# Eight of sixteen output tiles of w_out by one level of Strassen, in a fused transformer block on one Trainium2 core

## The chip, the cores and the metric

The kernel runs on one NeuronCore of one Trainium2 chip. The metric is the device time of one execution in microseconds. Five engines run side by side, each in the order of its own queue, and wait for one another through semaphores: TensorE (PE, matmuls; PEld its weight loads), VectorE (DVE), ScalarE (ACT), GpSimd (POOL, here used almost only to issue DMAs) and SyncE (SP, which only issues DMAs). All DMAs of the core run on its 16 DMA engines.

## The reference

A decoder block on 512 tokens with 2048 features, all in float32:

```python
x = x + jnp.concatenate([o_nsa, o_gla], axis=-1) @ w_out      # 2048 x 2048
hq = rms_norm(x, g_cross)
...                                                           # cross attention, 4 heads, 256 memory tokens
hf = rms_norm(x, g_ffn)
gg, uu = jnp.split(hf @ w_gu, 2, axis=-1)
return x + (jax.nn.silu(gg) * uu) @ w_down
```

`o_nsa` are eight sparse-attention heads and `o_gla` four gated linear-attention heads of two rows each: sixteen blocks of 128 features, the "mixed heads", which w_out projects back to 2048 features.

## The kernel before

**Precision.** Every large product is made of float32r matmuls on operands split in two: `split` writes hi = the rounded value (ACT) and lo = the rest (DVE). `mm3` then issues three matmuls, hi x hi, hi x lo and lo x hi, so a 128x128 block of weights against 512 tokens is three matmuls of 512 columns, each with its own weight load. All matmuls of helpers stand at one line, L109, and all splits at L196.

**Order of the program.** Memory keys and values, the projections of the combined input with the heads of both groups running between them, w_out, cross attention, then the feed-forward, whose two products (w_gu, w_down) already use one level of Strassen. A class `Flows` runs the heads as generators beside the projections: `tick()` counts one step, one every two contraction blocks of a projection, and resumes whatever is due. The order on each engine is then set by the framework's scheduler.

**Sums in DRAM.** Strassen needs sums of weight quarters. For w_down (`td`) and the first block of w_gu (`gu0`) POOL makes them in DRAM: a DMA copies a quarter, later ones add into it (`accum_op`). These are 120 DMAs in `turns`, sorted by a number that spreads each family, and given to the ticks 70 to 576 evenly. Each waits for the last matmul issued before its tick (L152 to L176), so POOL's queue runs in step with PE. `spill` and the loads of mixed heads are in the same queue.

**w_out.** `mixp` holds the sixteen mixed heads split, in 32 rows of the tag X. Heads that were spilled are loaded back in rows KS (L1057). L1070 projects the sixteen output tiles one by one: a tile is 16 contraction blocks x 3 = 48 matmuls, its weights two halves of 128x1024, each loaded by SP (4 raw buffers `w`) and split (3 buffers `wh`, 3 `wl`). L1080 adds the tile to x (`xs[m]`), L1085 and L1086 square it and add the square to `ss`, and `split_row` multiplies by g_cross and splits the row (`x1g`, L198 and L199) for the next projection, w_cq. The memory keys (`ckt`, `ckp`) are loaded and split at tiles 4 and 8. After w_out, `cross_norm` sums `ss` over features with PE, and `cross_head` runs four heads.

## Time and profile before

| | |
|---|---|
| median of three runs | 2292.02 us (2290.96 to 2294.07) |
| profiled execution | 2292.03 us, its span 2290.2 us |
| PE, DVE, ACT busy | 2281.0, 1653.3, 1179.4 us |
| heads end, w_out (729 to 891 us) | PE busy all of 162 us, DVE 68, ACT 51 |
| cross attention (891 to 915 us) | PE 23.83 of 24, DMA share 0.24 |

A busy time is the union of the engine's instructions; matmuls overlap in the pipeline, so their spacing is read from their starts. A row of a group gives count, busy time, mean ns of one, and the idle time before them with what ended it. In the chain of waits, the work that ended last is followed back, and its shares say which engine the program waited for. Times of the views are microseconds from the start of the span.

### The profile page before, as it was taken

Reading aid. Unit: us, or ns where it says so; the run is one execution under the profiler, and the core shown is the slowest. Engines: PE = TensorE matmul, PEld = TensorE weight load, DVE = VectorE, ACT = ScalarE, POOL = GpSimd, SP = SyncE. Lnnn points to the kernel's source line nnn. Section 1 sums busy time; section 2 is a strip of 40 time slices with the busy share of each in tenths; the row PEclk is TensorE's granted clock in tenths of the full one; section 3 lists DMA queues with packets and bytes.
Section 4 is the critical chain, followed back from the end, with each engine's and each line's share of the span. In section 5 each row is a group of like instructions: output and inputs, shape, how many; then the busy total and the mean of one; then the engine's idle time right before and its main releaser. Section 6 shows DMA issues by size and latency. Waiting matters only on the chain.

```text
span 2290.2 us, 29462 instructions
## 1 busy us (share of the span) xinstructions
PE 2281.0 (100%) x10800; PEld 1894.1 (83%) x10800; DVE 1653.3 (72%) x2525; ACT 1179.4 (51%) x1802; POOL 149.7 (7%) x200
## 2 busy tenths in 40 slices
PE   9999999999999999999999999999999999999999
PEld 7898888888887888788888888888888888888887
DVE  7548886666778335588788778878887886775685
ACT  7534454556667224475455445544554565444442
POOL 0011121111112110020000000000000000000000
PEclk9999999999999999999999999999999999999999
DMA  8587677856559773295445545543554497767674
GB/s 300 175 209 184 157 188 208 220 159 151 156 142 276 209 188 100 89 271 193 148 142 188 166 136 168 179 161 125 174 175 142 160 339 265 246 235 249 233 248 147
DMA packets 143441, 435.22 MB, mean 190 GB/s; under 512 B 14688, under 2 KB 35808, under 8 KB 140352
## 3 DMA queue, kind: packets, MB, share of 16 engines
q1 hardware_dynamic: 90832, 329.69, 42.4%
q0 software_dynamic: 28896, 79.18, 15.8%
q10 hardware_dynamic: 23568, 24.47, 3.0%
q8 instruction: 84, 1.38, 0.2%
q14 instruction: 61, 0.50, 0.1%
HBM read 394.75 MB, written 101.45 MB: 217 GB/s over the span
## 4 chain that ended last, share of the span: by engine, by line
PE 95%; DVE 2%; DMA 1%; ACT 1%; issue 1%; SPq 0%; ACTq 0%; DVEq 0%
PE mm L109 50%; PE t L109 18%; PE s L109 14%; PE o L109 11%; PE t L988 1%; PE s L1366 1%; DMA raw<-w_gu 1%; DVE wl L196 0%; DVE ql L196 0%; DMA st<-x_t 0%; PE t L1556 0%; ACT wh L196 0%; DMA PH<-w_ck 0%; ACT e L1129 0%; PE t L976 0%
## 5 line engine op out<-in xcount | busy, mean ns | idle before, releaser
L196 ACT CAST qh<-raw 128x1024 fp32r<-128x1024 f32 (+1 forms) x494 | 477.9, 976 | 513.8 <-PE o L109 168.7
L196 DVE TENSOR_TENSOR ql<-raw,qh 128x1024 fp32r<-128x1024 f32 (+1 forms) x494 | 553.7, 1127 | 145.9 <-PE mm L109 55.6
L109 PE MATMUL mm<-X,wh 128*128 128x512 f32 x1664 | 525.1, 395 | 0.0
L109 PEld LDWEIGHTS mm<-X,wh 128*128 128x128 f32 x1664 | 305.4, 188 | 60.0 <-issue 2.2
L109 PE MATMUL t<-qh,PB 128*128 128x512 f32 x968 | 334.9, 391 | 0.0
L109 PE MATMUL mm<-X,wl 128*128 128x512 f32 x832 | 326.2, 392 | 0.2
L196 DVE TENSOR_TENSOR wl<-w,wh 128x1024 fp32r<-128x1024 f32 (+2 forms) x172 | 205.8, 1202 | 163.3 <-ACT wh L196 162.6
L196 ACT CAST wh<-w 128x1024 fp32r<-128x1024 f32 (+2 forms) x172 | 176.6, 1032 | 270.3 <-PE mm L109 177.1
L109 PE MATMUL mm<-qh,PB 128*128 128x512 f32 x868 | 309.8, 389 | 0.0
L109 PE MATMUL s<-qh,PB 128*128 128x512 f32 x672 | 232.6, 391 | 0.6 <-ACT qh L196 0.6
L109 PE MATMUL mm<-qh,PA 128*128 128x512 f32 x640 | 221.5, 389 | 0.0
L109 PEld LDWEIGHTS t<-qh,PB 128*128 128x128 f32 x968 | 181.7, 188 | 37.1
L109 PEld LDWEIGHTS mm<-qh,PB 128*128 128x128 f32 x868 | 163.0, 188 | 34.0 <-ACT qh L196 0.2
L109 PE MATMUL t<-ql,PB 128*128 128x512 f32 x484 | 188.3, 389 | 0.0
L109 PE MATMUL o<-qh,PB 128*128 128x512 f32 x484 | 187.4, 389 | 0.0
L109 PEld LDWEIGHTS mm<-X,wl 128*128 128x128 f32 x832 | 156.2, 188 | 34.0 <-DVE wl L196 1.5
L109 PE MATMUL mm<-ql,PB 128*128 128x512 f32 x434 | 169.0, 389 | 0.1
L109 PEld LDWEIGHTS s<-qh,PB 128*128 128x128 f32 x672 | 126.0, 188 | 26.8 <-ACT qh L196 1.3
L109 PEld LDWEIGHTS mm<-qh,PA 128*128 128x128 f32 x640 | 120.1, 188 | 25.2
L109 PE MATMUL s<-ql,PB 128*128 128x512 f32 x336 | 131.4, 391 | 0.1
L109 PE MATMUL mm<-ql,PA 128*128 128x512 f32 x320 | 124.5, 389 | 0.0
L1299 DVE TENSOR_TENSOR raw<-raw 128x1024 f32<-128x1024 f32 x80 | 96.9, 1220 | 17.7 <-DMA raw<-w_gu 17.7
(486 smaller groups left out, 3388.3 us busy)
## 6 DMA issues: line engine op xcount, KB each, us to landing
raw<-w_gu SPq DMA_DIRECT2D x80, 768.0 KB, 4.1
raw<-w_down SPq DMA_DIRECT2D x88, 512.0 KB, 4.7
raw<-w_gu SPq DMA_DIRECT2D x80, 512.0 KB, 3.5
td<-w_down POOLq DMA_DIRECT2D x66, 512.0 KB, 7.1
w<-w_a SPq DMA_DIRECT2D x60, 512.0 KB, 5.8
raw<-td SPq DMA_DIRECT2D x22, 1024.0 KB, 5.0
HR<-h SPq DMA_DIRECT2D x35, 512.0 KB, 4.9
h<-T ACTq DMA_DIRECT2D x66, 256.0 KB, 3.7
```

Source lines behind the costliest of these rows:

```text
L109: last_mm[0] = PE.matmul(*args, **kw)
L196: last_split[:] = S.copy(hi, src), V.tensor_sub(lo, src, hi)
L988: PE.transpose(tp[:, 128 * (i - j):128 * (i - j) + 128], ps_[b][:, POFF[i] + 128 * j:POFF[i] + 128 * j + 128], ident)
L1299: V.tensor_add(raw[:, 0:1024], raw[:, 0:1024], raw[:, 512:1536])
L1366: PE.transpose(ps[f][:, 128 * i:128 * i + 128], hs[i][:, c:c + 128], ident)
```

## The change

The first eight output tiles are projected as before (`w_o8`). The last eight form two units, u = 2 and 3, of four tiles each. In a unit the contraction (blocks in pairs, the even and the odd head of a pair), the output tiles (pairs) and the tokens (halves of 256) are each cut in two, and seven products replace eight: product `a` takes one quarter of the weights, plain or summed, for two output tiles `i`, against one quarter or sum of quarters of the mixed heads, 256 tokens wide. Results gather in four PSUM banks (`b1`, `b2`, `b3`, `bu`); products 1, 6 and 2 add on to what a bank holds, after `add_22` has read it.

The weight quarters come in a new layout, `w_out`, of four tiles in DRAM with quarters side by side. Their sums (`wo`) are made in DRAM by POOL, 32 more DMAs in `turns`, which now has 152 entries over the ticks 70 to 600. The four sums of the mixed heads (`fac`) are made on chip: every mixed head is spilled, `load_mixes` loads a pair of blocks back on POOL's queue, `mix_sums` makes the sums on DVE and splits them. The places of `mixp`, `fac` and `x1g` are shared by a table (`PLACE`); the x1g rows of the first eight tiles are made during the units, and the memory keys are loaded after the units and split in the first cross head. Heads 4 and 5 use rows st in place of M and are spilled and loaded back too.

```diff
+FIRST_SUM, LAST_SUM = 70, 600
+    wo = [dram.tile([128, 4096], F32, name="wo", tag="wo", bufs=4) for b in range(4)]
+    def add_half(b, h, k):
+        d, w = wo[b][:, 2048 * h:2048 * h + 2048], w_out[b, :, 2048 * h:2048 * h + 2048]
+        def go():
+            if k == 0:
+                i = G.dma_start(d, w)
+            else:
+                dst, src = ((d[:, 512:1536], w[:, 1024:2048]), (d[:, 1536:2048], d[:, 512:1024]),
+                            (d[:, 0:512], d[:, 1536:2048]))[k - 1]
+                i = G.dma_start(dst, src, accum_op=OP.add, max_dma_last_dim=2048)
...
-    turns += [((4 * kp + k + 0.9) / (4 * KP), add_block(kp, k)) for kp in range(KP) for k in range(4)]
+    turns += [((4 * kp + 5.1 * k + 0.9) / (4 * KP + 16), add_block(kp, k)) for kp in range(KP) for k in range(4)]
+    turns += [((2 * b + h + 1.3 * k + 0.2) / 14.5, add_half(b, h, k)) for b in range(4) for h in range(2) for k in range(4)]
...
+    def factor_of(a, kp):
+        if a < 3:
+            return part(mixp[2 * kp + (a > 0)], 256 * (a == 2), 256)
+        return part(fac[a, kp // 2], 256 * (kp % 2), 256)
+    def load_mixes(*kps):
+        for kp in kps:
+            mixes[kp] = [row(tag) for tag in (("M", "rs") if kp % 2 else ("n", "ss"))]
+            for h in range(2):
+                G.dma_start(mixes[kp][h], saved[MIX_ORDER[2 * kp + h]])
+    def mix_sums(*kps):
+        for kp in kps:
+            a0, a1, b0, b1 = [t[:, 256 * i:256 * i + 256] for t in mixes[kp] for i in range(2)]
+            for a, op, d, x, y in ((3, V.tensor_sub, b1, b1, a1), (5, V.tensor_sub, a1, a0, a1),
+                                   (4, V.tensor_add, a0, b1, a0), (6, V.tensor_sub, b0, a0, b0)):
+                op(d, x, y)
...
+                split(*factor_of(a, kp), d)
...
+    def out_weights(src):
+        with tc.high_priority(offset=OUT_AHEAD):
+            raw = sb([128, 1024], "w", 4)
+            nc.sync.dma_start(raw.rearrange("p (h c) -> p h c", h=2), src)
+            hi, lo = sb([128, 1024], "wh", 3, F32R), sb([128, 1024], "wl", 3, F32R)
+            split(hi, lo, raw)
+    def unit(u, a):
+        q, dst, summed = {0: (3, b1, 0), 1: (0, b1, 0), 3: (2, b3, 1), 5: (1, b2, 1), 4: (3, bu, 1), 6: (1, b3, 0),
+                          2: (0, b2, 1)}[a]
...
+        for i in range(2):
+            b = 2 * u - 4 + i
+            w = out_weights((wo[b] if summed else w_out[b])...[:, :, 512 * q:512 * q + 512])
+            for kp in range(KP):
+                mm3(dst[u][:, 256 * i:256 * i + 256], part(w, 128 * kp, 128), factor_of(a, kp), ...)
+                if kp % 4 == 3:
+                    flows.tick()
...
+    def add_22(u):
+        n = ns[u] = spare_n[u % 2]
+        V.tensor_sub(n, bu[u], us[u])
+        V.tensor_sub(t, n, b2[u])
+        V.tensor_sub(t, t, b3[u])
...
+    def finish_x1(u, *ks):
+        for k in ks:
+            m = 4 * u + k
...
+            split(*x1g[m], xs[m], vec("g_cross", m))
+            if m:
+                sq = sqs[k % 2]
+                S.activation(sq, xs[m], AF.Square)
+                V.tensor_add(ss, ss, sq)
...
-    for m in range(KT):
-        ps = project(Weights(w_out[m], 2048), mixp)
...
+    for m in range(8):
+        V.tensor_add(xs[m], project(Weights(w_o8[m], 2048), mixp), xs[m])
+        for at, go, g in ((2, load_mixes, 0), (3, mix_sums, 0), (3, load_mixes, 1), (5, mix_sums, 1),
+                          (5, load_mixes, 2), (6, mix_sums, 2)):
+            if m == at:
+                go(2 * g, 2 * g + 1)
+    for u in (2, 3):
+        unit(u, 0)
+        us[u] = row("M")
+        S.copy(us[u], b1[u])
+    load_mixes(6, 7)
+    unit(2, 1)
+    add_11(2)
+    mix_sums(6, 7)
...
+    unit(2, 3)
+    finish_x1(0, 0, 1)
+    unit(3, 3)
+    finish_x1(0, 2, 3)
+    unit(2, 5)
+    finish_x1(1, 0, 1)
+    unit(2, 4)
+    finish_x1(1, 2, 3)
+    unit(3, 5)
+    for u in (2, 3):
+        add_22(u)
+        unit(u, 6)
+        add_n(u)
+        add_21(u)
+        if u == 3:
+            finish_x1(3, 1, 3)
+        unit(u, 2)
+        add_12(u)
+        if u == 2:
+            unit(3, 4)
+            unit(3, 1)
+            finish_x1(2, 1, 3, 0, 2)
+            add_11(3)
+    finish_x1(3, 0, 2)
```

Three places show how the order moves. On PE, at the end of the eighth output tile, the next tile of 512 columns stood before (X are mixed heads, one hi and one lo row each; mm is a bank):

```order
L109 MATMUL mm_7586<-X_7034,wh_7582 128x512
L109 MATMUL mm_7586<-X_7035,wh_7582 128x512
L109 MATMUL mm_7586<-X_7034,wl_7583 128x512
L109 MATMUL mm_7656<-X_6974,wh_7646 128x512
L109 MATMUL mm_7656<-X_6975,wh_7646 128x512
L109 MATMUL mm_7656<-X_6974,wl_7647 128x512
L109 MATMUL mm_7656<-X_6978,wh_7646 128x512
```

Now unit 2's first product stands there, 256 columns wide, over every second head:

```order
L110 MATMUL mm_7694<-X_7076,wh_7690 128x512
L110 MATMUL mm_7694<-X_7077,wh_7690 128x512
L110 MATMUL mm_7694<-X_7076,wl_7691 128x512
L110 MATMUL mm_7746<-X_7016,wh_7749 128x256
L110 MATMUL mm_7746<-X_7017,wh_7749 128x256
L110 MATMUL mm_7746<-X_7016,wl_7750 128x256
L110 MATMUL mm_7746<-X_7024,wh_7749 128x256
```

Three matmuls per block stay three, at half the columns, and each still brings its own weights.

On POOL, the DRAM sums of the time around the eighth tile's end stood alone before (td for w_down, gu_112 for w_gu):

```order
L173 DMA gu_111<-gu_111 128x512
L154 DMA td<-td 128x2x512
L156 DMA td<-w_down 128x1024
L169 DMA gu_112<-w_gu 16x16384
L154 DMA td<-td 128x2x512
```

Now a load of a spilled mixed head (M) stands between them; it belongs to the last two block pairs, and the td row ahead of it is the sum of tick 530:

```order
L191 DMA wo<-wo 128x512
L155 DMA td<-td 128x2x512
L157 DMA td<-w_down 128x1024
L155 DMA td<-td 128x2x512
L157 DMA td<-w_down 128x1024
L155 DMA td<-td 128x2x512
L1103 DMA M<-spill 128x512
L174 DMA gu_112<-gu_112 128x512
```

The last sum of `wo` stands six rows ahead of that load.

On DVE, in w_out before, a tile's addition, a square's addition and two weight splits alternate:

```order
L196 TENSOR_TENSOR wl_7653<-w_7650,wh_7652 128x1024
L1080 TENSOR_TENSOR KV_7056<-mm_7586,KV_7056 128x512
L196 TENSOR_TENSOR wl_7724<-w_7721,wh_7723 128x1024
L1086 TENSOR_TENSOR ss_7070<-ss_7070,n_7637 128x512
L196 TENSOR_TENSOR wl_7730<-w_7727,wh_7729 128x1024
```

In the units, the last mix (rs, M), its split (X_7947), the rows of x1g (X_8043) and the additions out of a bank (KV, on) stand between the weight splits:

```order
L215 TENSOR_TENSOR wl_7983<-w_7980,wh_7982 128x1024
L215 TENSOR_TENSOR X_7962<-ss_7875,X_7961 128x256
L218 SCALAR_TENSOR_TENSOR X_8043<-KV_7090,vecs_117,X_8042 128x512
L1110 TENSOR_TENSOR rs_7879<-rs_7879,M_7878 128x256
L215 TENSOR_TENSOR wl_8014<-w_8011,wh_8013 128x1024
L215 TENSOR_TENSOR X_7947<-rs_7879,X_7946 128x256
L1110 TENSOR_TENSOR M_7878<-M_7878 128x256
L218 SCALAR_TENSOR_TENSOR X_8048<-q1_7110,vecs_117,X_8047 128x512
L1159 TENSOR_TENSOR KV_7086<-mm_7746,KV_7086 128x256
L1159 TENSOR_TENSOR on_7112<-mm_7746,on_7112 128x256
L215 TENSOR_TENSOR wl_8057<-w_8054,wh_8056 128x1024
```

The weight split wl_8014 and all behind it now stand behind the subtraction that needs the M load.

More of the change, by code (lines that the diff above doesn't have):

```diff
@@ L63, in hybrid_block @@
 def hybrid_block(ctx: ExitStack, tc: tile.TileContext, x_t, mem_t, sv, cmat, umask, w_a, w_r67, w_v, w_vg, w_v3,
-                 w_vsw, w_gk2, w_c1, w_c2, w_out, w_cq, w_ck, w_cv, w_co, w_gu, w_down, y_t):
+                 w_vsw, w_gk2, w_c1, w_c2, w_o8, w_out, w_cq, w_ck, w_cv, w_co, w_gu, w_down, y_t):
     nc = tc.nc
@@ L1007, in nsa_head @@
         done.add(("a", h))
-        t = row("st" if h < 4 else "M")
+        t = row("st" if h < 6 else "M")
         S.copy(t, o)
@@ L1015, in nsa_head @@
         V.scalar_tensor_tensor(t, t, vec("g_nsa"), r, op0=OP.mult, op1=OP.mult)
-        mix[h] = spill(t) if h < 4 else t
+        saved[h] = spill(t)
+        mix[h] = saved[h] if h < 6 else t
     us = short_rows(10)
@@ L1035, in swish_gate @@
         V.tensor_mul(r1, r1, e)
-        V.tensor_mul(t, t, r1)
-        mix[8 + m] = spill(t) if m < 6 else t
+        d = t if m < 6 else row("M")
+        V.tensor_mul(d, t, r1)
+        saved[8 + m] = spill(d)
+        mix[8 + m] = saved[8 + m] if m < 6 else d
     for n in IN_ORDER:
@@ new lines, in hybrid_block @@
+    b1, b2, b3, bu, us, ns = {}, {}, {}, {}, {}, {}
+    def unit(u, a):
+        q, dst, summed = {0: (3, b1, 0), 1: (0, b1, 0), 3: (2, b3, 1), 5: (1, b2, 1), 4: (3, bu, 1), 6: (1, b3, 0),
+                          2: (0, b2, 1)}[a]
+        again = a in (1, 6, 2)
+        if not again:
+            dst[u] = bank({0: "mm", 3: "s", 5: "t", 4: "o"}[a])
+        for i in range(2):
+            b = 2 * u - 4 + i
+            w = out_weights((wo[b] if summed else w_out[b]).rearrange("p (h c) -> p h c", h=2)
+                            [:, :, 512 * q:512 * q + 512])
+            for kp in range(KP):
+                mm3(dst[u][:, 256 * i:256 * i + 256], part(w, 128 * kp, 128), factor_of(a, kp),
+                    start=not again and kp == 0 and i == 0, stop=kp == KP - 1 and i == 1, again=again)
+                if kp % 4 == 3:
+                    flows.tick()
@@ new lines, in columns, with add_11 @@
+    def columns(u):
+        for i in range(2):
+            yield xs[4 * u + 2 * i], xs[4 * u + 2 * i + 1], slice(256 * i, 256 * i + 256)
+    T0, T1 = slice(0, 256), slice(256, 512)
+    def add_11(u):
+        for x, _, c in columns(u):
+            V.tensor_add(x[:, T0], b1[u][:, c], x[:, T0])
+    spare_n, t = [row("on"), row("on")], row("q1")
+    def add_22(u):
[3 more added lines that the diff above has]
+        V.tensor_sub(t, t, b3[u])
@@ new lines, in add_n, with add_21, add_12 @@
+    def add_n(u):
+        for x, y, c in columns(u):
+            V.tensor_add(y[:, T0], y[:, T0], ns[u][:, c])
+            V.tensor_sub(x[:, T1], x[:, T1], ns[u][:, c])
+            V.tensor_add(y[:, T1], y[:, T1], t[:, c])
+    def add_21(u):
+        for _, y, c in columns(u):
+            V.tensor_sub(y[:, T0], y[:, T0], b3[u][:, c])
+    def add_12(u):
+        for x, _, c in columns(u):
+            V.tensor_add(x[:, T1], b2[u][:, c], x[:, T1])
+    ss = row("M")
+    x1g = [None] * KT
@@ L1090, in hybrid_block, with memory_keys @@
+    finish_x1(3, 0, 2)
+    ckt, cv = [row("X") for _ in range(2)], [row("X") for _ in range(2)]
+    for i in range(2):
+        G.dma_start(ckt[i], memkv["k", i])
+        G.dma_start(cv[i], memkv["v", i])
+    ckp = []
+    def memory_keys():
+        for a in range(2):
+            ckp.append(split_row(ckt[a]))
     oc = []
@@ L1349, in phase @@
             weights(kp)
+            flows.tick()
             for p in last if kp == KP - 1 else middle:
```

67 lines of the change are left out of this document (38 added, 29 removed).

## The prediction

> **What bounds the kernel now.** I read the first part of the page, then the chain of waits, then the table by stage.
>
> ```profile
> span 2290.2 us, 29462 instructions
> PE 2281.0 (100%) x10800; PEld 1894.1 (83%) x10800; DVE 1653.3 (72%) x2525; ACT 1179.4 (51%) x1802; POOL 149.7 (7%) x200
> PE 95%; DVE 2%; DMA 1%; ACT 1%; issue 1%; SPq 0%; ACTq 0%; DVEq 0%
> 729.00:775.00 46.00, 46.00 (x203) 37.64 (x202) 19.93 (x24) 14.59 (x18) 8.42 (x10) 1.00 0.89 233
> 775.00:820.00 45.00, 45.00 (x201) 37.26 (x200) 14.97 (x16) 10.54 (x12) 6.64 (x8) 1.00 0.75 202
> 820.00:860.00 40.00, 40.00 (x178) 33.15 (x177) 13.75 (x15) 9.85 (x12) 6.41 (x8) 1.00 0.71 189
> 860.00:891.00 31.00, 31.00 (x140) 25.56 (x138) 19.31 (x25) 16.16 (x23) 0.85 (x1) 1.00 0.45 114
> ```
>
> TensorE is the bound: 95% of the chain is PE work. The last four rows are the w_out stage, columns PE, PEld, DVE, ACT, POOL (busy us and count), granted clock, DMA share, GB/s. PE has no idle time there, the clock is full, and DVE and ACT are under half busy until the last 31 us. So a matmul that disappears here shortens the program by its spacing, as long as nothing new starves PE.
>
> A busy time of 0.39 us is not the spacing of pipelined matmuls; that is read from start to start.
>
> ```profile
> 98.48 0.40 PE L109 MATMUL t<-wh,X 128*128 128x256 f32 x2
> 112.87 0.40 PE L109 MATMUL t<-wh,X 128*128 128x256 f32 x2
> 879.80 0.39 PE L109 MATMUL mm<-X,wl 128*128 128x512 f32 x1
> 890.68 0.39 PE L109 MATMUL mm<-X,wl 128*128 128x512 f32 x1
> 887.03 0.69 DVE L1080 TENSOR_TENSOR KS<-mm,KS 128x512 f32<-128x512 f32 x1
> ```
>
> The first pair lies 40 groups of three matmuls apart, all 256 wide, each with its own weight load, in the same hi-hi-lo pattern: 14.39 / 120 = 0.120 us each. The second pair lies 16 groups of three apart, 512 wide: 10.88 / 48 = 0.2267 us. One output tile of w_out has 48 of these, 10.88 us. The last row evicts the sixteenth tile, so that tile ends at 886.9 and the eighth at 886.9 - 8 x 10.88 = 799.9.
>
> **The matmuls.** The last eight tiles go: 8 x 48 = 384 at 0.2267 = 87.0 us. In come two units of seven products; a product is 2 tiles x 8 pairs of contraction blocks x 3 = 48 matmuls of 256, 5.76 us: 672 at 0.120 = 80.6 us. That is 6.4 us less. Seven eighths would be 10.9 us less; 4.5 us of it goes because half-width matmuls cost 53% and not 50%. Everything else can only take away from 6.4.
>
> **Feeding the units.** Before, a half tile of weights lasts PE 5.44 us; now it lasts 24 x 0.120 = 2.88. The stage needs 28 loads and splits of 128x1024 in 80.6 us, where 16 stood in 87.0.
>
> ```profile
> L196 DVE TENSOR_TENSOR wl<-w,wh 128x1024 fp32r<-128x1024 f32 (+2 forms) x172 | 205.8, 1202 | 163.3 <-ACT wh L196 162.6
> L196 ACT CAST wh<-w 128x1024 fp32r<-128x1024 f32 (+2 forms) x172 | 176.6, 1032 | 270.3 <-PE mm L109 177.1
> 710.50 0.42 DVE L196 TENSOR_TENSOR PL<-t,PH 128x256 fp32r<-128x256 f32 x1
> 709.78 0.35 ACT L196 CAST PH<-t 128x256 fp32r<-128x256 f32 x1
> 883.64 3.39 DVE L199 SCALAR_TENSOR_TENSOR X<-KV,vecs,X 128x512 fp32r<-128x512 f32 x5
> 890.10 0.69 DVE L1086 TENSOR_TENSOR ss<-ss,n 128x512 f32<-128x512 f32 x1
> ```
>
> DVE in the 80.6 us: 28 x 1.20 = 33.6 for the weights; the mixes of the last two block pairs, 8 sums and 8 splits at 0.42 = 6.7; per unit three 512-wide ops at 0.69 and twelve 256-wide at 0.42, together 14.2; sixteen x1g splits at 0.68 and fifteen additions of squares at 0.69 = 21.2. Sum 75.7 us, 94%; it was about a third of the time. ACT: 28 x 1.03 + 8 x 0.35 + 34 ops of 512 at about 0.65 = 54 us. DVE fits, with 5 us to spare, but it runs in order: what waits for a product holds the weight splits behind it, and only three split halves (8.6 us) stand before PE. Bounds 0 and 5 us.
>
> The same for DMA.
>
> ```profile
> q0 software_dynamic: 3515, 9.18, 36.1%
> q1 hardware_dynamic: 3200, 11.61, 29.4%
> w<-w_out SPq DMA_DIRECT2D x15, 512.0 KB, 4.5
> q0 software_dynamic: 2217, 6.06, 53.7%
> q1 hardware_dynamic: 2444, 6.52, 39.4%
> w<-w_out SPq DMA_DIRECT2D x9, 512.0 KB, 6.3
> td<-td POOLq DMA_DIRECT2D x4, 512.0 KB, 11.3
> q0 software_dynamic: 3649, 9.70, 56.4%
> q1 hardware_dynamic: 2624, 9.13, 30.9%
> w<-w_a SPq DMA_DIRECT2D x17, 512.0 KB, 8.0
> ```
>
> The DMA view of 770 to 890, then of 720 to 770 (four rows), the last three of 130 to 220; q0 is POOL's queue of DRAM sums, q1 SP's weights. From the first two rows half a megabyte costs 120 x 0.361 / 17.5 = 2.5 us of all 16 engines on q0 and 120 x 0.294 / 22.1 = 1.6 us on q1. The units ask for 28 x 1.6 = 44.6 us of weights (55%), and the DRAM sums, one per 3.49 ticks instead of 4.22, for about 15 x 2.5 = 37 us (46%). That is 101%: the transfers run full. What helps is depth: four raw buffers, so a half comes every (landing + 1.03 + 1.20) / 4 us, and 2.88 is kept up to a landing of 9.3 us. The median landing was 8.0 under a share of 87% (130 to 220) and 6.3 under 93% (720 to 770). Bounds 0, and at a landing of 11 us 28 x 0.43 less the 8.6 us that stand split, 3.4 us. The DMA and DVE limits overlap; I take 0.6 us for both, near the rows of 6.3 and 8.0, which cost nothing.
>
> **The mixes on POOL's queue.** Sixteen loads of mixed heads are new, in order among the sums, each of which waits for PE's tick. One is late: the M row of the last two block pairs, behind the sum due at tick 530.
>
> ```profile
> 801.74 1.19 POOL L154 DMA_DIRECT2D td<-td  x1 [5.06 <-PE mm L109]
> 807.05 0.54 POOL L156 DMA_DIRECT2D td<-w_down  x1 [4.12 <-PE mm L109]
> 744.12 1.16 POOL L173 DMA_DIRECT2D gu<-w_gu  x1 [13.86 <-issue]
> 761.22 1.14 POOL L154 DMA_DIRECT2D td<-td  x1 [14.21 <-PE mm L109]
> KS<-spill POOLq DMA_DIRECT2D x8, 256.0 KB, 3.5
> st<-spill POOLq DMA_DIRECT2D x6, 256.0 KB, 7.5
> ```
>
> The 807.05 row is the 110th of 120 sums, due at tick 529; a tick of w_out is 1.36 us, so the eighth tile ends at tick 524. In the units a tick is 12 x 0.120 = 1.44 us: tick 530 comes 8.6 us after the eighth tile, the td issue takes 1.2, M's own 0.5, and the load lands 3.5 to 7.5 us later (last two rows, 640 to 720): 13.8 to 17.8 us. The fourth product's first half needs the sum made from it at 17.28 + 2.52 = 19.8, less a subtraction, a cast, a split and their handovers, 1.5 us: 18.3. So there is 0.5 to 4.5 us of slack if POOL is on time. Its queue was 14 us behind at 744 and 761, and on time from 784 on. If late, ACT and DVE both stand at this mix with the weight splits behind them, and PE follows one for one. I take 0.5 us; bounds 0 and 11.
>
> **Ends and covers.** The sum of squares must now wait for two additions, two splits and two squares after the last product; DVE order puts a weight split between: 2 x 0.42 + 1.20 + 2 x (0.68 + 0.69) and handovers, about 5.2 us, where PE has 22 matmuls, 5.0 us, in front of it. Before it waited 0.19 us:
>
> ```profile
> 890.84 0.97 PEld L109 LDWEIGHTS s<-vecs,ss 128*128 128x128 f32 x8 [0.19 <-DVE ss L1086]
> 640.00:729.00 89.00, 88.91 (x463) 72.66 (x461) 73.64 (x191) 67.69 (x144) 19.73 (x30) 1.00 0.72 200
> ```
>
> I take 0.3 (0 to 1.3). The mixes of the first block pairs are made among the heads, 16 DVE ops of 0.42 and 8 casts for a pair of them, where DVE is 83% and ACT 76% busy; PE's order there is unchanged and its idle 0.1 us in 89, so 0.2 (0 to 1.5). Splitting the memory keys in the first cross head instead of under w_out is 2 x 0.68 on DVE under 10.9 us of the next w_cq tile: 0.1 (0 to 0.5). The other mixes, the eight DRAM tiles' 32 sums and the extra spills cost nothing before 800 us while the weights there last 5.44 us per half; without that cover they are the rivals below.
>
> **Sum.** -6.4 + 0.6 + 0.5 + 0.3 + 0.2 + 0.1 = -4.7 us. The profiled execution took 2292.03, its span 2290.2 and 1.8 around it; it stands at the median of 2292.02. Span 2285.5, time 2287.3.
>
> **Rivals.** (1) Weights late, chance 0.18: DMA at 101% lets landings reach 10 to 12 us, PE waits 3 to 6 us at every second product, the gain is gone: about 2290, no change. For it the sum of demands, against it 720 to 770, where 93% cost PE nothing.
>
> (2) M late, the case on the other side, chance 0.18: the POOL queue is still behind when the eighth tile ends, since between the first w_out tile and tick 530 it has 23 sums where 19 stood, and twelve mixes. Behind by the 14 us of the 744.12 row, M lands 9.5 to 13.5 us late and the time is -5.2 + 11.5 = 6.3 over, 2298. It decides from a landing 18.3 us after the eighth tile, and turns slower at about 23.5. Against it: at 801 and 807 POOL waited for PE, not for the ring.
>
> (3) Weight loads pace the narrow matmuls, 0.02. Each unit matmul has a load that takes 188 ns:
>
> ```profile
> L109 PEld LDWEIGHTS mm<-X,wh 128*128 128x128 f32 x1664 | 305.4, 188 | 60.0 <-issue 2.2
> ```
>
> At that spacing 672 x 0.188 = 126.3, 39 us over 87.0: 2331. The 0.120 above, with as many loads, speaks against it. The Trainium skill (TensorE: Matmul & The Clock Gate, section Back-to-back issue gap) says that loads and matmuls together set the spacing, 81 ns at 128 columns and 131 at 512; read as a straight line that is some 98 at 256, 75% of a full one, and as an estimate the units would then take 113.7 us and the time rise by 27 to 2319. The trace does not agree: 0.120 against 0.2267 is 53%.
>
> (4) The added work among the heads and the early weights costs more than I think (DVE 83%, DMA 0.72 and more), 0.06: 2 to 8 us, 2290 to 2295.
>
> **How the numbers follow.** The forecast has 0.56; its own range, all covers holding or two of the small terms at their upper bound, is 2285.6 to 2289. A measurement of this kernel tells about 0.2%, 4.6 us, from no change, and the forecast lies on that line: 0.45 faster, 0.11 same. Rival 1: 0.01, 0.12, 0.05. Rival 2: same 0.08, slower 0.10. Rival 3 slower. Rival 4: 0.03 and 0.03. Together 0.46 faster, 0.34 same, 0.20 slower. The range for 8 in 10 runs from 2285.0, a little under all covers holding, to 2295.5, into rivals 1, 2 and 4.
>
> **What would show it.** Right: 672 matmuls 0.36 us per three, the units about 81 to 83 us from the eighth tile's end, w_cq's first matmul 5 to 6 us sooner than 886.9. Rival 1: PE idle on wh or wl at many halves, w landings of 10 us and more. Rival 2: one gap of several us in the fourth product, ACT and DVE idle on the M load, POOL's td issues there late against their ticks. Rival 4: the eighth tile ends later than 799.9. I am wrong in the mechanism if PE has no gaps in the units and the stage is still not shorter.

## The result, and the profile after

The changed kernel takes 2317.42 us, median of four runs (2316.72 to 2318.70), beside 2292.12 for the kernel before on the same chip: a ratio of 1.0109, 95% interval 1.0097 to 1.0122. That is 25.3 us slower, where 4.7 us faster was forecast and the range ended at 2295.5. The profiled execution took 2317.08 us, its span 2315.3.

First the page of the changed kernel (span, engines, chain by engine).

```profile
span 2315.3 us, 30388 instructions
PE 2284.6 (99%) x11088; PEld 1910.4 (83%) x11088; DVE 1694.9 (73%) x2623; ACT 1204.7 (52%) x1848; POOL 191.2 (8%) x256
PE 66%; DMA 2%; issue 1%; DVE 1%; ACT 0%; POOL 0%; POOLq 0%; DVEq 0%; ACTq 0%
```

288 matmuls more, as seven products for eight at half width make it. The shares of the chain add up to about 70% here and to 100% before, so the chain does not account for the whole span and the two cannot be compared engine by engine. The table by stage tells where the time goes (columns as in the prediction: length, busy us and count of PE, PEld, DVE, ACT, POOL, granted clock, DMA share, GB/s; the DMA share adds up the times of packets, so it can come out above 1).

```profile
640.00:700.00 60.00, 59.91 (x317) 50.03 (x317) 47.91 (x145) 42.23 (x96) 13.63 (x20) 1.00 0.61 163
700.00:770.00 70.00, 52.03 (x221) 41.34 (x220) 43.39 (x90) 37.11 (x74) 22.91 (x33) 0.85 0.92 259
770.00:825.00 55.00, 55.00 (x244) 45.53 (x244) 23.42 (x38) 13.65 (x19) 11.87 (x16) 1.00 0.86 222
825.00:912.00 87.00, 84.31 (x676) 83.75 (x675) 66.46 (x96) 48.96 (x67) 16.76 (x22) 0.96 0.92 247
```

And the same of the kernel before, the second of these stretches:

```profile
700.00:770.00 70.00, 70.00 (x328) 56.57 (x327) 44.56 (x78) 38.23 (x67) 16.37 (x22) 1.00 0.95 273
```

PE stands for 18 us between 700 and 770 us, where the last heads end and w_out begins, and for 2.7 us in the units. The DMA engines were as full there before (0.95) as after (0.92), and PE did not stand. So the load on the DMA engines alone does not explain it; something now waits for a DMA that did not before.

Before looking at what, the three stalls and the one in the units more closely, in shorter stretches of the same table:

```profile
700.00:705.50 5.50, 0.49 (x3) 0.06 (x1) 0.99 (x2) 1.58 (x3) 0.13 (x2) 0.88 0.93 284
705.50:710.00 4.50, 4.31 (x12) 3.53 (x13) 3.05 (x6) 2.57 (x6) 1.73 (x4) 0.50 0.37 118
736.00:743.50 7.50, 0.38 (x2) 0.00 (x0) 1.33 (x4) 0.97 (x3) 2.75 (x5) 0.66 1.07 351
743.50:749.00 5.50, 5.49 (x14) 4.35 (x15) 4.24 (x8) 3.87 (x7) 1.00 (x2) 0.54 1.07 267
754.00:759.00 5.00, 0.00 (x0) 0.00 (x0) 3.21 (x8) 1.29 (x3) 1.13 (x3) 0.98 1.03 283
849.00:853.00 4.00, 4.00 (x21) 4.00 (x20) 4.00 (x9) 3.06 (x6) 0.00 (x0) 0.50 0.57 171
```

PE is idle from start to start of its matmuls for 5.5 us at 700, 7.3 at 736, 5.5 at 753 and 3.2 at 845 us (there 2.3 and 0.9 with one matmul between). After each of them the granted clock is near one half for 3 to 6 us (0.50, 0.54 and 0.50 in the rows behind the first, second and fourth): the 256-wide matmuls then come every 0.21 us, not 0.12, and the 512-wide every 0.43, not 0.2267. So each stall costs about 2 us beyond its own length.

What each of them waits for, from the waits of 640 to 912 us (waiting instruction, releaser: us in total, times, longest) and, of the second, the timeline of POOL, DVE, ACT and PE:

```profile
DVE rs L1110 <- DMA M<-spill: 12.8, 2, 7.0
DVE ss L1110 <- DMA n<-spill: 7.5, 1, 7.5
ACT st L215 <- DVE ss L1110: 7.2, 1, 7.2
PE t L110 <- ACT on L215: 7.1, 1, 7.1
ACT X L215 <- DMA KS<-spill: 6.8, 2, 5.8
```

```profile
731.21 0.55 POOL L1103 DMA_DIRECT2D n<-spill  x1
742.07 0.42 DVE L1110 TENSOR_TENSOR ss<-ss,n 128x256 f32<-128x256 f32 x1 [7.48 <-DMA n<-spill]
742.53 0.41 ACT L215 CAST st<-ss 128x256 fp32r<-128x256 f32 x1 [7.21 <-DVE ss L1110]
742.84 0.61 ACT L215 CAST on<-on 128x512 fp32r<-128x512 f32 x1
743.51 0.79 PE L110 MATMUL t<-on,ones_r 128*128 128x512 f32 x1 [7.13 <-ACT on L215]
```

Read from the last row up: PE wants the split square (`on`) of a head. The square had been ready since 735.3 us. Its split stands on ACT behind the split of a mixed head's sum (`st<-ss`), that waits for DVE's subtraction (L1110, `mix_sums`), and that for a load of a mixed head (L1103) which POOL issued at 731.21 and which was there 10.9 us later. Nothing in this chain is needed by PE before the units begin 80 us later, except the last link. The stall at 753 us is of the same kind (a load of M, issued at 742.58, was there at 755.8). The one at 700 us is ACT at the split of a head that is loaded back (`X` from KS), with the split of a score block (`PH`) behind it. The last has the shape of rival 2 of the prediction:

```profile
835.39 1.14 POOL L155 DMA_DIRECT2D td<-td  x1 [6.14 <-PE mm L110]
836.10 1.05 POOL L1103 DMA_DIRECT2D M<-spill  x1
836.10 10.30 DMA M<-spill
```

Two rows of POOL's timeline and one of the chain of waits: the load of M is issued behind the w_down sum and lands 10.3 us later.

The units run from the first 256-wide matmul to the first of w_cq, 86.5 us, in place of 87.0:

```profile
825.35 0.40 PE L110 MATMUL mm<-X,wh 128*128 128x256 f32 x2
911.87 0.63 PE L110 MATMUL mm<-X,wh 128*128 128x512 f32 x2
```

They begin at 825.35 where 799.9 was the eighth tile's end before, 25.4 us late; so the whole loss lies ahead of them and their own gain is eaten inside.

### The profile page after: what moved, and what is told of

Read it like the earlier page. It is cut to its first block, busy times and chain, and to the rows that moved or that the text cites. A ratio compares the mean times of both kernels' runs of the same rounds, so it can differ in the third digit from the quotient of the medians.

```text
span 2315.3 us, 30388 instructions
## 1 busy us (share of the span) xinstructions
PE 2284.6 (99%) x11088; PEld 1910.4 (83%) x11088; DVE 1694.9 (73%) x2623; ACT 1204.7 (52%) x1848; POOL 191.2 (8%) x256
## 4 chain that ended last, share of the span: by engine, by line
PE 66%; DMA 2%; issue 1%; DVE 1%; ACT 0%; POOL 0%; POOLq 0%; DVEq 0%; ACTq 0%
PE mm L110 29%; PE t L110 16%; PE s L110 12%; PE o L110 8%; DMA M<-spill 1%; PE s L1526 1%; DMA KS<-spill 0%; PE t L1716 0%; PE t L1302 0%; DMA td<-w_down 0%; POOL td L155 0%; DVE wl L215 0%; ACT e L1288 0%; ACT wh L215 0%; PE t L1526 0%
## 5 line engine op out<-in xcount | busy, mean ns | idle before, releaser
L110 PE MATMUL mm<-X,wh 128*128 128x512 f32 (+1 forms) x1464 | 449.6, 388 | 5.3 <-ACT X L215 5.3
L215 DVE TENSOR_TENSOR wl<-w,wh 128x1024 fp32r<-128x1024 f32 (+2 forms) x184 | 220.5, 1203 | 147.6 <-ACT wh L215 145.1
L215 ACT CAST wh<-w 128x1024 fp32r<-128x1024 f32 (+2 forms) x184 | 189.1, 1032 | 231.0 <-PE mm L110 156.5
L110 PEld LDWEIGHTS mm<-X,wh 128*128 128x128 f32 x1464 | 266.2, 190 | 51.0 <-ACT X L215 5.8
L110 PE MATMUL mm<-X,wl 128*128 128x512 f32 (+1 forms) x732 | 282.0, 385 | 0.2 <-DVE wl L215 0.2
L110 PEld LDWEIGHTS mm<-X,wl 128*128 128x128 f32 x732 | 138.9, 190 | 28.4 <-DVE wl L215 1.5
L1458 DVE TENSOR_TENSOR raw<-raw 128x1024 f32<-128x1024 f32 x80 | 96.8, 1220 | 15.7 <-DMA raw<-w_gu 15.7
```

The costliest lines, as they stand in the source:

```text
L110: last_mm[0] = PE.matmul(*args, **kw)
L215: last_split[:] = S.copy(hi, src), V.tensor_sub(lo, src, hi)
L1458: V.tensor_add(raw[:, 0:1024], raw[:, 0:1024], raw[:, 512:1536])
```

## The experiments

All times are medians with the ratio to the kernel before on the same chip (2291.8 to 2292.6 us on those used) and its 95% interval; the other columns are read from the PE timeline of each profile: where the last head's norm is summed, where the units begin, and how long they are.

| kernel | us | ratio (interval) | last head | units begin | units, us |
|---|---|---|---|---|---|
| before (tiles 9 to 16 for the units) | 2292.1 | 1 | 728.7 | 799.9 | 87.0 |
| the change | 2317.4 | 1.0109 (1.0097 to 1.0122) | 745.4 | 825.4 | 86.5 |
| e1 no w_out sums in DRAM | 2313.1 | 1.0087 (1.0069 to 1.0106) | 743.1 | 820.9 | 85.3 |
| e2 late w_down sums in the gated layer | 2329.2 | 1.0158 (1.0143 to 1.0173) | 737.2 | 813.4 | 80.6 |
| e3 mixed loads and sums after their tile | 2312.4 | 1.0085 (1.0070 to 1.0101) | 734.4 | 817.3 | 88.0 |
| e4 the units alone | 2288.7 | 0.9980 (0.9971 to 0.9990) | 729.1 | 799.3 | 80.6 |
| e5 mixed sums from pairs on chip | 2293.5 | 1.0009 (0.9999 to 1.0018) | 734.6 | 804.5 | 80.6 |
| e6 the units and the w_out sums | 2294.6 | 1.0008 (0.9999 to 1.0018) | 731.5 | 801.7 | 80.6 |
| e7 reloads on SP's queue | 2316.0 | 1.0104 (1.0089 to 1.0119) | 738.4 | 821.4 | 84.2 |
| e8 mixed sums alone after their tile | 2305.4 | 1.0061 (1.0044 to 1.0078) | 734.9 | 807.3 | 91.8 |
| e9 pairs, one per tile, sums later | 2289.6 | 0.9987 (0.9978 to 0.9996) | 733.7 | 803.9 | 80.6 |
| e10 as e6, two more heads reloaded | 2303.6 | 1.0044 (1.0030 to 1.0057) | 737.0 | 809.4 | 80.6 |
| e11 as e9, w_out sums later still | 2287.2 | 0.9983 (0.9975 to 0.9992) | 730.1 | 800.3 | 80.6 |
| e12 as the change, last load first | 2316.4 | 1.0112 (1.0096 to 1.0127) | 745.6 | 824.5 | 82.7 |

The theories that the expectations name. **Theory 1**: the stalls come from loads that land late and from the sums that stand in line for them on DVE and ACT, both together. **Rival A**: the 32 new sums in DRAM fill the DMA engines. **Rival B**: the place in line alone. **Rival C**: the units do not pay on PE. **Theory 2**, after the first four runs: reloads late on POOL's queue with engines in line behind them; the units are good for 6.4 us. **Rival D**: DVE is too full. **Rival E**: the DMA engines are full, whatever queue is used.

### e1 to e4: what the loss is not, and the units alone

**e1**, the change without the 32 sums, the products read `w_out[b]`:

```diff
-        flows.marks.append((FIRST_SUM + n * (LAST_SUM - FIRST_SUM) // len(turns), go))
+        if go.__qualname__.split('.')[-3] != 'add_half':
+            flows.marks.append((FIRST_SUM + n * (LAST_SUM - FIRST_SUM) // len(turns), go))
-            w = out_weights((wo[b] if summed else w_out[b])...
+            w = out_weights(w_out[b]...
```

> The changed kernel without the 32 DRAM sums of w_out: the products that take summed weights read unsummed blocks of w_out of the same size, so the output is not the reference's; the other sums keep their ticks. In the changed kernel PE stands three times between 699 and 760 us (5.5, 7.3 and 5.5 us) and once in the units (3.2 us). Theory 1 (loads of mixed heads that land late, with their sums in line on DVE and ACT; both the full DMA queues and the place in line are needed): landings get shorter but not short, the three stalls shrink by about half, 2303 (2298 to 2309). Rival A (the 32 sums alone fill the DMA engines): all three stalls go, 2288 to 2293. Rival B (the place in line alone): 2314 to 2318. Rival C (the units do not pay on PE): the stage from the first product to the first w_cq matmul stays 86 us or more even without a gap; the others say 81 to 83 without a gap.

2313.1: 4.4 us less than the change, and all four stalls are still there (5.6, 7.8, 3.4 and 3.3 us). Rival A falls as the cause of the stalls; theory 1 expected 2303 and was too hopeful, and the time lies nearest to rival B's 2314 to 2318.

**e2**, the w_down sums due late moved into the gated layer:

```diff
+        at = FIRST_SUM + n * (LAST_SUM - FIRST_SUM) // len(turns)
+        if at >= 390 and go.__qualname__.split('.')[-3] == 'add_quarters':
+            late.append((630 + 3 * len(late), go))
```

> The changed kernel with the w_down sums that were due from about 640 us on (34 of 88) moved to ticks of the gated FFN layer; all else as it is, w_out's sums too. It takes some 34 sums at 2.5 us of all 16 engines out of 640 to 945 us, more than the 32 w_out sums took there. Theory 1: POOL no longer waits 7 to 8 us for room in its queue, landings of mixed heads fall to 4 to 6 us, the stalls shrink to 2 us each or go, and the last load is no longer behind a w_down sum, so its 3.2 us go too: 2293 (2287 to 2300). Rival A (the 32 w_out sums alone): 2305 or more, since those stay. Rival B (the place in line alone): 2311 to 2315, only the gap in the units goes.

2329.2, and all theories missed it, because of what the moved sums did where they went. Up to w_cq it is in part as theory 1 has it: two stalls instead of four, no gap in the units, w_cq at 894.0 instead of 911.9. The stall at 700 us is down to 2.0 us, but one of 6.9 is left at 743, where theory 1 had 2 at most. The loads of mixed heads land sooner; those into M, first in the change (725 to 754 us), then in e2 (719 to 747):

```profile
M<-spill POOLq DMA_DIRECT2D x2, 256.0 KB, 13.1
```

```profile
M<-spill POOLq DMA_DIRECT2D x3, 256.0 KB, 7.8
```

The DMA share of 720 to 760 us falls from 1.01 to 0.72 with it, so the sums of w_down have a part in the late landings, and rival B, the place in line alone, falls. Then the gated layer and w_down take 29.9 us more. Its rows of 1060 to 1860 us, first of the change, then of e2, each followed by the loads of w_gu between 1200 and 1600 us (count, size, median us to landing):

```profile
1060.00:1860.00 800.00, 799.87 (x3601) 661.74 (x3601) 647.96 (x788) 408.92 (x510) 0.00 (x0) 1.00 0.48 159
raw<-w_gu SPq DMA_DIRECT2D x40, 768.0 KB, 4.1
```

```profile
1060.00:1860.00 800.00, 779.43 (x3462) 634.49 (x3462) 626.05 (x760) 390.46 (x491) 33.43 (x39) 1.00 0.58 179
raw<-w_gu SPq DMA_DIRECT2D x40, 768.0 KB, 5.5
```

The DMA engines are 42% idle there, and still PE stands for 20 us: the loads land 1.4 us later, and DVE's first operation on these weights waits for them 50.4 us in all, where it waited 15.7 in the change.

**e3**, loads and with them sums of the first six pairs behind their w_out tile (`last_mm[0]` is that tile's last matmul):

```diff
-                G.dma_start(mixes[kp][h], saved[MIX_ORDER[2 * kp + h]])
+                i = G.dma_start(mixes[kp][h], saved[MIX_ORDER[2 * kp + h]])
+                if kp < 6:
+                    tc.add_manual_dep(i.ins, last_mm[0].ins.name, ...)
```

> The changed kernel, but the twelve loads of mixed heads for the first six block pairs each wait for PE's last matmul of the w_out tile behind which the program has them (tiles 2, 3 and 5); with that their sums also stand behind those tiles on DVE and ACT. The DMA work is the same. Theory 1: the stalls at 736 and 753 us go with the half clock behind them (7.3 + 5.5 + 2 x 2.3 = 17 us), the one at 700 us, which is a reload of a head, stays: 2300 (2297 to 2304). Rival A (the DMA engines are full whatever stands in line): 2311 to 2318. Rival B (the place in line alone): 2292 to 2300. A loss in the w_out tiles, where DVE and ACT now stand at the mixes, would show as new gaps between 770 and 830 us.

2312.4, where theory 1 had 2300 and rival A 2311 to 2318. The stalls at 736 and 753 are gone and the last head ends at 734.4, but one of 7.4 us has come at 769, another kind of the same:

```profile
DVE ss L1114 <- DMA ss<-spill: 22.3, 2, 19.4
PEld mm L110 <- DVE wl L215: 7.7, 1, 7.7
```

DVE stands 19.4 us at the first sum, with the rest of a weight split (`wl`) behind it, and PE waits for that. Moving load and sum together moves the stall. The units take 7.3 us more than 80.6 too: the last load is issued 16.9 us after they begin.

**e4**, the units with nothing that feeds them: no calls of `load_mixes` and `mix_sums`, no extra spills, not the 32 sums, and heads 4 to 7 in M as before the change:

```diff
-        return part(fac[a, kp // 2], 256 * (kp % 2), 256)
+        return part(mixp[2 * kp + a % 2], 256 * (a // 2 % 2), 256)
```

> The two units without what feeds them: no sums of w_out in DRAM, no extra spills, loads and sums of mixed heads; every product reads unmixed heads and unsummed blocks of w_out, so the output is not the reference's, but PE runs the same 672 matmuls and DVE the same additions behind them, and heads 4 to 7 stay on chip as before the change. All theories but C: no stall among the heads, the units 81 to 83 us, 2286 to 2289, 4 to 6 us faster than the kernel before. Rival C (units of half-width matmuls do not pay in this place): 2291 or more, with the pitch of three matmuls above 0.36 us or DVE in their way.

2288.7, faster than before. PE does not stand in the units; they take 80.63 us:

```profile
799.32 0.40 PE L110 MATMUL mm<-X,wh 128*128 128x256 f32 x2
879.95 0.63 PE L110 MATMUL mm<-X,wh 128*128 128x512 f32 x2
```

Rival C falls. The 6.4 us of the matmuls are there to the tenth.

### e5 to e8: the loads, the queue and the place in line

**e5**, the mixed heads' sums from the split pairs that are on chip, main parts and rests apart (the diff shows b1 - a1); no extra spill or load:

```diff
-                G.dma_start(mixes[kp][h], saved[MIX_ORDER[2 * kp + h]])
+                V.tensor_sub(A0, b1[0], a1[0])
+                V.tensor_sub(B0, b1[1], a1[1])
+                V.tensor_add(A0, A0, B0)
```

In this kernel one of the four sums has the opposite sign, which changes the output and no work.

> The changed kernel, but the mixed heads' sums are made from the split pairs that are on chip (main part and rest apart, 10 additions of 256 columns for a pair of blocks instead of 4), so the 16 extra spills and 16 loads are gone and heads 4 to 7 stay on chip as before the change. The 32 sums of w_out in DRAM and all ticks stay. Theory 2 (reloads that come late on POOL's queue, with DVE and ACT in line behind them, are the loss; the units themselves are good for 6.4 us): no gap above 1 us from 640 to 900 us, the units 81 to 83 us, 2287 (2285 to 2291); the 48 further additions are 20 us of DVE in tiles where it is under half busy. Rival A (the 32 sums in DRAM, not the loads): gaps stay, 2300 or more. Rival D (DVE's further work among heads and in units): gaps where PE waits for wl, 2292 to 2300.

2293.5: 24 us less than the change. No gap above 1 us lies between 640 and 900 us, the units take 80.6. It misses 2287 by 6.5 us, most of them lost long before: compared matmul by matmul with the kernel before it is 2.8 us behind from 160 us on and 3.9 from 400 on, and 4.6 when the units begin. So although the time lies in the range of rival D (2292 to 2300), DVE's further work among the heads costs 0.7 us at most.

**e6**, e4 with the sums in DRAM, which the products read:

> The units alone again (no spills, loads or sums of mixed heads; every product reads unmixed heads, so the output is not the reference's), but with the 32 sums of w_out in DRAM and the products that read them. Beside the run without those sums (2288.7; units 80.6 us) it prices the sums by themselves. Theory 2: nothing to 2 us, 2286 to 2291, the units 80.6 to 83. Rival A: 2295 or more, with weights that land late in the units (the DMA engines were reckoned at 101% there) or among the heads.

2294.6, 5.9 us more than e4: above theory 2's 2286 to 2291 and just under rival A's 2295. The sums by themselves take back the units' gain. The first place where they cost is at 150 us, as in the change. The row of that stretch in the kernel before, then in the change, then in e6 with what it waits for:

```profile
140.00:165.00 25.00, 24.96 (x135) 21.66 (x134) 16.41 (x45) 11.38 (x19) 5.14 (x6) 1.00 0.84 215
```

```profile
140.00:165.00 25.00, 23.48 (x123) 19.61 (x122) 15.29 (x42) 10.92 (x17) 2.88 (x3) 1.00 1.04 296
```

```profile
140.00:165.00 25.00, 23.63 (x124) 19.79 (x124) 14.95 (x41) 10.92 (x17) 2.88 (x3) 1.00 1.03 296
ACT wh L215 <- DMA w<-w_a: 5.7, 2, 4.0
```

The DMA share goes from 0.84 to 1.03 and a weight load is late by 4 us. That is 1.7 us against e4. It does not come in every execution: e3 and e8, with the same sums due at the same ticks and shares of 1.05 and 1.04 in this stretch, have PE busy for 24.96 of the 25 us. In e6 another 0.8 goes at 400, and 3.9 between the units and the gated layer, 2.6 of it one gap where the memory keys' load is late, behind a w_down sum on POOL's queue. The run without the sums, e1, gave 4.4 us; I read 4 to 6. (The gated layer and w_down take 1266.4 to 1270.0 us in these profiles without order among the kernels, e2 left out, so a difference under 4 us in one profile's end says nothing.)

**e7**, the reloads issued by SP instead of POOL:

```diff
-                G.dma_start(mixes[kp][h], saved[MIX_ORDER[2 * kp + h]])
+                nc.sync.dma_start(mixes[kp][h], saved[MIX_ORDER[2 * kp + h]])
-            G.dma_start(t, mix[k])
+            nc.sync.dma_start(t, mix[k])
```

> The changed kernel with the same spills, loads and sums, but the reloads of heads and of mixed heads are issued on SP's queue, among the weights, instead of POOL's, where sums of 512 KB stand ahead of them. Theory 2: the loads land in 3 to 6 us; the stall at 700 us shrinks to 2 us or less, those at 736 and 753 us shrink or go, the gap in the units goes: 2296 (2290 to 2303). Rival E (the DMA engines are full whatever queue is used): landings of 7 us and more, 2310 to 2318. Against both: loads that wait for their rows on SP hold the weights behind them, which would show as PE waiting for wh.

2316.0, where theory 2 said 2296. The stall at 700 us shrinks to 1.0 and 1.2 us and the gap in the units to 1.1 and 0.9 with one matmul between, as it said; but 3.1 us at 730 and 9.1 us at 744 have come in place of the other two. The chain there:

```profile
730.05 12.44 DMA KV<-x_t
742.55 13.39 DMA ss<-spill
```

On SP's own queue, with no sum ahead of it, a load of 256 KB takes 13.4 us; ahead of it are loads of x_t, and one of these takes 12.4. For these loads rival E is right: being behind the sums in POOL's queue is not what makes them late. Yet the kernel before, with a DMA share of 0.95 from 700 to 770 us, shows that PE need not stand when the engines are that full.

**e8**, loads as in the change, only the first sum of a pair waits for its tile:

```diff
-                op(d, x, y)
+                i = op(d, x, y)
+                if kp < 6 and a == 3:
+                    tc.add_manual_dep(i.ins, last_mm[0].ins.name, ...)
```

> The changed kernel with loads as they are, but the sums of mixed heads of the first six block pairs wait for the last matmul of the w_out tile behind which the program has them, so that on DVE and ACT they stand behind the last head and not in front of its norm; the loads of the first two pairs are then long there. Theory 2: the stalls at 736 and 753 us go with their half clock (17 us), the one at 700 us (5.5 + 2.3) and the one in the units (3.2 + 2.3) stay: 2300 (2297 to 2304). Rival E: DMA late in any place, 2308 or more, with new waits on loads in the w_out tiles.

2305.4, where theory 2 said 2300. The stalls at 736 and 753 us are gone with the DMA engines as full as they were. The stretch from 712 us on, of the change and of e8:

```profile
712.00:770.00 58.00, 45.23 (x200) 36.11 (x199) 37.66 (x79) 31.23 (x63) 19.63 (x28) 0.88 0.98 268
```

```profile
712.00:770.00 58.00, 57.70 (x273) 46.62 (x272) 38.21 (x70) 30.48 (x54) 17.85 (x23) 1.00 0.99 278
```

The units begin at 807.3, 18 us sooner than in the change; 1.6 of these 18 lie ahead of 712 us, so the two stalls are worth 16.4, and theory 2 said 17. So these two stalls need the place in line: late loads alone do not make PE stand. But 11.2 us are lost in the units (two gaps of 1.8 and 4.7 us at 810 and 815, and half clock), because the third group's loads can only start when the second group's sums have freed the rows (793.5 us), land 11 us later, and DVE stands again:

```profile
805.49 0.43 DVE L1110 TENSOR_TENSOR ss<-ss,n 128x256 f32<-128x256 f32 x1 [7.64 <-DMA ss<-spill]
```

### e9 to e12: the two heads, the last load, and a better version

**e10**, e6 with heads 4 and 5 spilled and reloaded as in the change (`row("st" if h < 6 else "M")`, `spill(t) if h < 6 else t`):

> The units with the w_out sums but without mixed heads, as in the run before (2294.6; the output is not the reference's, every product reads unmixed heads), and heads 4 and 5 spilled and reloaded as in the changed kernel: 12 reloads of heads instead of 10. If the two reloads on POOL's queue, behind head 5's spill and a w_down sum, are what makes PE stand at 700 us, the gap of about 5.5 us is back there with 4 to 5 us of half clock behind it: 2300 to 2303. If that stall needs the mixed heads' loads as well (more DMA, more in POOL's queue), there is no gap above 2 us and the time stays at 2293 to 2296.

2303.6, 9.0 us more than e6. The profile has the stall back at 700 us, 5.2 us, the only one, and the units begin 7.7 us later than in e6:

```profile
ACT X L215 <- DMA KS<-spill: 6.6, 2, 5.8
PE o L110 <- ACT PH L215: 4.8, 1, 4.8
```

So it takes no mixed head to make it. The first reload is issued 0.6 us later than in e6 (694.17 for 693.57), behind head 5's spill. The three after it now stand right behind a w_down sum on POOL's queue, issued at 695.5 to 696.6; first these three, then the four reloads of e6 from 693 to 702 us:

```profile
KS<-spill POOLq DMA_DIRECT2D x3, 256.0 KB, 8.2
```

```profile
KS<-spill POOLq DMA_DIRECT2D x4, 256.0 KB, 3.0
```

In e2, which has the two heads' reloads but not that w_down sum, the stall is 2.0 us. The profiled execution is this kernel's quickest, 2296.6; the other three took 2303 to 2304, and what they lost beyond it no trace shows.

**e12**, the change with the two w_down sums due at ticks 525 to 539 moved to tick 540:

```diff
+        at = FIRST_SUM + n * (LAST_SUM - FIRST_SUM) // len(turns)
+        flows.marks.append((540 if 525 <= at < 540 else at, go))
```

> The changed kernel, but the two w_down sums due at ticks 525 to 539, the last of which stands ahead of the last load of a mixed head on POOL's queue, come at tick 540, behind that load. If that sum and its wait for PE's tick are what makes the load late (issue at 836.1 us, landed at 845 to 847 us), the gap of 3.2 us in the fourth product and the 2.3 us of half clock behind it go and the units take 80.6 to 82 us instead of 86.5: 2312 (2310.5 to 2314.5). If the load is late for another reason (landing of 10 us whatever stands ahead), units of 85 us or more and 2315 to 2318.

The load of M is issued at 824.85 and the gap in the fourth product is gone, the clock full; the units take 82.7 us instead of 86.5. The 2.1 us above 80.6 are mostly two pauses, 1.0 and 0.8 us, ahead of each unit's product 6, where PE waits for DVE (`add_22`).

```profile
824.85 1.05 POOL L1104 DMA_DIRECT2D M<-spill  x1
```

So without the two w_down sums ahead of it the load is issued 11.3 us sooner and is there in time. In the time it is not to be seen: the profiled execution took 2313.9 us and the change's 2317.1, but the median, 2316.4, is above the 2310.5 to 2314.5 expected and only 1 us below the change's, and this kernel's own runs lie 5.7 us apart.

**e9**, the version that the runs pointed to: e5 with the sign mended, one block pair's sums behind each of tiles 1 to 6, and the 32 sums between ticks 260 and 440, the other 120 at the ticks of the kernel before:

```diff
+    halves = [add_half(b, h, k) for b in range(4) for k in range(4) for h in range(2)]
+    flows.marks.extend((SUM_O + n * (LAST_O - SUM_O) // len(halves), go) for n, go in enumerate(halves))
...
+        if 1 <= m <= 6:
+            load_mixes(m - 1)        # rows only, nothing is loaded
+            mix_sums(m - 1)          # the first subtraction waits for tile m's last matmul
```

> The version that the runs so far point to: mixed heads' sums from the split pairs on chip (the last of the four with its sign mended), no extra spills or loads, heads 4 to 7 on chip as before the change; the sums of each of the first six block pairs wait for one of the w_out tiles 1 to 6, one pair per tile, so that none stands in front of a head on DVE; the 32 sums of w_out in DRAM lie between ticks 260 and 440 instead of from tick 70 on, and the other 120 sums keep the ticks that they had before the change. Theory 2: the losses at 150 and 400 us (0.8 to 2.8 us together) and among the heads (3.9 us where the sums stood as the scheduler liked) go, the units keep 80.6 us: 2286.5 (2284.5 to 2289), about 0.998 of the kernel before. If the 32 sums cost their 5 us wherever they stand, 2291 or more. If DVE is too full in the w_out tiles (its work there goes from 26 to some 60 us in 87), gaps at wl of the tiles and 2290 or more.

2289.6, ratio 0.9987, just above the range expected (to 2289). Nothing is lost at 150 and 400 us, nor between 500 us and the end of the units; but the sums have found another place to hurt, 4.2 us at 450, where the chain has

```profile
438.40 13.40 DMA w<-w_a
```

**e11**, the same with the sums between ticks 296 and 456:

```diff
-SUM_O, LAST_O = 260, 440
+SUM_O, LAST_O = 296, 456
```

> As the version with all mixed heads' sums on chip (2289.6), but the 32 sums of w_out in DRAM between ticks 296 and 456 (from about 460 us on) instead of 260 to 440: there, three 512 KB sums at 441 to 443 us stood in the way of a w_a load that landed after 13.4 us, PE stood 2.5 us at 450 us and the kernel ran 4.2 us behind from there on. If it is the place of the sums beside the w_a loads that costs, those 4.2 us go and nothing comes in their place: 2285.5 (2283.5 to 2288). If 32 sums cost some us in any place of a DMA load of 0.6 to 0.9, a new gap comes at reloads or weights between 460 and 720 us and the time stays at 2288 to 2291.

2287.2, ratio 0.9983 (0.9975 to 0.9992): 0.2% faster than the kernel before, and faster than the change. PE does not stand anywhere between 640 and 910 us, as in these rows of e11 (700 to 740, w_out, units):

```profile
700.00:740.00 40.00, 40.00 (x196) 31.80 (x195) 31.90 (x66) 28.71 (x55) 12.48 (x17) 1.00 1.04 302
740.00:800.00 60.00, 60.00 (x266) 49.73 (x265) 49.95 (x106) 20.24 (x35) 10.25 (x12) 1.00 0.87 226
800.00:881.00 81.00, 81.00 (x675) 80.92 (x675) 68.32 (x103) 48.49 (x67) 13.09 (x16) 1.00 0.92 257
```

The DMA share of 1.04 in the first row is as high as in the stalls of the change (0.93 to 1.07). With no mixed head's load in line, it costs PE nothing. The units begin at 800.3, 0.4 us behind the kernel before.

## Why the prediction was wrong

**The matmuls, -6.4: right.** 80.6 us for 672 of them in seven kernels (e2, e4, e5, e6, e9, e10, e11), as worked out, where eight tiles took 87.0. Rival 3 is out: its 0.188 us each would have made 126.3. Nor did the estimate of 113.7 us come that the prediction made from the Trainium skill (TensorE: Matmul & The Clock Gate, section Back-to-back issue gap).

**Feeding the units, 0.6: nothing.** In those kernels PE has no gap in the units, at a DMA share of 0.92 in e11 and 0.97 in e4, with DVE busy 68 of 81 us in e11, which makes even more additions than the change. The 101% was an upper estimate, and rival 1 did not come. The room on DVE is small: in the units of e12 PE does wait for it, 1.8 us.

**The last load, 0.5: mis-sized, 5.9.** Place and timing were right: the issue came 10.8 us after the eighth tile's end (8.6 + 1.2 + 0.5 predicted) and PE stood from 19.8 us after it, as worked out. What was wrong is the landing, taken as 3.5 to 7.5 us from rows at a DMA share of 0.72; it took 10.3. That is 3.2 us of stall and some 2.7 of half clock (86.5 against 80.6), inside the bound of 11. Rival 2 thus came by another door than it named: POOL was on time, the load was slow. In e3 the door was the one it named: POOL issued the load 16.9 us after the units began, and it landed in 5.8. In e12, where the load is issued 11.3 us sooner, there is no gap behind it.

**The ends, 0.4: nothing.** From the first w_cq matmul to the first of the gated layer's products it is 132.3 us, 132.2 before.

**The step that failed** is "the other mixes, the eight DRAM tiles' 32 sums and the extra spills cost nothing before 800 us", with the 0.2 for the mixes among the heads ahead of it, "PE's order there is unchanged and its idle 0.1 us in 89". In its place the profile shows 25.4 us lost ahead of the units. The prediction made that step hold as long as weights last 5.44 us per half; but none of the three stalls ahead of the units waits for a weight. By the medians the way from the kernel before to the change is -3.4 (units alone), +5.9, +9.0 and +13.8. By the ratios, which take out the chip, it is -4.6, +6.4, +8.3 and +14.9, so each part is known to about 1 us at best:

- The sums in DRAM: 4 to 6 us (e6 against e4, e1 against the change), at 150 and 400 us and, in e6, behind the units. In the profile of the change the first two places are 2.9 us. I had weighed their DMA time against the units alone, although they begin at tick 70, beside w_a's loads; the stretch of 130 to 220 us that I took as one where a full DMA costs nothing is the first where they cost something.
- The two heads spilled and loaded back: 9.0 us (e10 against e6), a stall of 5.2 us with its half clock in the profile. I had counted the spills as work that something hides, and not looked at which reloads then stand behind a w_down sum on POOL's queue.
- The mixed heads' loads and sums: the rest, 13.8 us from e10 to the change, the last load's 5.9 included; and 24 us between the change and e5, where both the loads and the two heads' reloads are gone. I had priced the sums as 16 DVE operations of 0.42 us and 8 casts. The cost is not their work but what they wait for, with a head's norm and a weight split behind them in the order of DVE and ACT. e8 shows it: the two stalls go when the sums alone stand elsewhere. e2 shows that the loads' lateness is the other half: with the late w_down sums gone, two of the four stalls go and one shrinks.

Rival 4 named the place (2 to 8 us, chance 0.06), and its test (the eighth tile later than 799.9) is met, at 825.4; its size was a third of what came, for the same reason: it too was worked out from busy shares.

My expectations in the runs missed in the same direction. Taking one late thing away (e1, e3, e7) left another in the same line, and moving work to a stage that looked idle (e2) cost more there than it saved. What stays open: why a load of 256 KB takes 10 to 13 us at 725 to 850 us while the median of such loads elsewhere was 3.5 to 7.5. e7 excludes the sums ahead in its own queue as the only cause, and e2 brings the loads into M from 13.1 to 7.8 us by taking the late w_down sums off the DMA engines, so these are a part of it; the rest no run isolates. Open is also how the 13.8 us split between the stalls, since each depends on the one before, and why the loss at 150 us is missing in some executions.

## What to carry to other kernels

Price an operation that is added to an engine in order not by its own time but by when its last input lands, and read in the engine's order what stands behind it: a sum that nobody needs for 80 us held PE for 7 us because it stood ahead of one that was needed at once. Data that is on chip, even split in two, was worth 2.5 times the additions here, since it saved a reload in a stretch where the DMA engines are full. Background DMAs have to be placed by whether the foreground loads have slack there, not by the idle share of the engines: the same 32 sums cost 4 to 6 us in one place and about nothing in another, and 34 sums cost 30 us beside loads with a DMA share of 0.48.

## What the hardware showed that I had not expected

A gap on PE costs more than itself. After 2.5 us of idle (e9 at 450 us) and after 3.2 in two pieces (the change at 845) the granted clock fell to about one half for 3.4 and 5.9 us, 0.21 us for a 256-wide matmul and 0.43 for a 512-wide. After 2.0 us (e2 at 700) the spacing was full again within a matmul, yet after two pauses of 1.1 and 0.9 us in the units of e7 it was half as well:

```profile
843.90:847.30 3.40, 3.40 (x19) 3.40 (x18) 3.40 (x8) 2.58 (x5) 0.00 (x0) 0.50 0.76 192
```

So the length of a gap alone does not tell whether it comes. With four stalls it is some 8 of the 30 us between the forecast and the result, in no term of the prediction. The Trainium skill (TensorE: Matmul & The Clock Gate, Part 1: The HAM clock gate) has such a half rate after an idle window of about 3.4 us, and the full rate again after about 3.4 us of work. The runs agree on the half; they had the full rate back after 3.0 to 5.9 us of work, and they show that a gap shorter than that window can already be enough.
